# Feeding an encoder layer a second, channel-major copy of its input: no transposes at the start, token sums by matmul, a longer warm-up

## The chip, the cores and the metric

The kernel runs on one core of one Trainium2 chip. The metric is the device time of one execution, in microseconds (us), as the median of several runs. The engines are called TensorE (PE, with its weight loads shown apart as PEld), VectorE (DVE), ScalarE (ACT), GpSimd (POOL) and SyncE (SP), which here issues the DMAs.

## What is computed

One layer of a bidirectional encoder on 256 tokens of 2048 channels. A normalisation, a five-part input projection, a gated recurrence over chunks in both directions, an output projection, and then a gated feed-forward block with a width-3 convolution; each half is added to its input.

```
def reference(x, ...):
    h = rmsnorm(x, norm_pre_mix[i])
    m = hgrn2_mixer(h, hgrn_w_in[j], hgrn_w_out[j], ...)
    x = x + rmsnorm(m, norm_post_mix[i])
    h = rmsnorm(x, norm_pre_ffn[i])
    x = x + rmsnorm(conv_ffn(h, ffn_w_in[i], ffn_w_conv[i], ffn_w_out[i]), norm_post_ffn[i])

def rmsnorm(x, w):
    y = x32 * lax.rsqrt(jnp.mean(x32 * x32, axis=-1, keepdims=True) + EPS)
    return (y * w).astype(x.dtype)
```

All of it is float32. The change concerns the first `rmsnorm` alone: how `x * norm_pre_mix` gets into the layout that the matmuls need, and how the mean square of each token is summed.

## The kernel before, in words

**The work.** The weights, 59 million values, stream from memory once. A product in float32 accuracy is made of fast ones: every weight piece `raw` is split into a rounded part `whi` (a cast on ACT, line 129) and a rest `wlo` (a subtraction on DVE, line 130), every activation likewise into two halves of the tile `xx[:, k, 0/1, :]`. Index `k` counts 16 blocks of 128 channels; the channels of a block lie on the 128 partitions, the 256 tokens along the free side.

**Chunks and steps.** The 2048 by 10240 input weights are taken in chunks of 512 columns. The function `gemm_t` computes a chunk in 8 steps; step `s` uses blocks `k = 2s, 2s+1`. In a step, 8 matmuls multiply `whi` with both halves of `xx` (512 columns, line 206), and 8 multiply `wlo` with the first half (256 columns, line 209). `prep` casts and subtracts the weights some steps ahead: one step in the first chunk, three (`LOOK`) from then on. The chunk's results stand in four PSUM tiles (`pg`) of six that there are, so the second chunk can take two at once, and gets the others when DVE has copied the first chunk's results away (lines 346 and 347).

**The start.** The input `x` arrives with tokens on partitions (`xs`, five DMAs), between the weights of the first chunk, all on SP's queue, in the order `x` 256 columns, weights k 0 and 1, `x` 256, weights k 2 and 3, `x` 512, weights k 4 to 7 (two DMAs), `x` 512, `x` 512, then weights in 1 MB pieces of four blocks. TensorE first does `WARM` = 18 transposes of the identity into a scratch tile. `split_x(k2)` then transposes two blocks of `xs` on TensorE (four 128 by 128 transposes, line 290), multiplies by the norm's weight on ACT (first half, line 294), and takes the rest on DVE (second half, line 298). `split_x(0)` and `split_x(1)` stand ahead of the first chunk; step `s` calls `split_x(s + 2)`.

**The mean square.** ACT squares `xs` and sums along the channels in the same instruction (`square_x`, eight calls, line 309). DVE adds the eight partial sums, GpSimd takes the power -0.5 (`rsqrt_mean`), and `spread` brings the result across the partitions with two matmuls (line 222). The factors `rs1` (per partition) and `r1` (per column) are applied to the results of the projection, not to `xx`. These pieces are put into the list `soon`; each step of a chunk takes one piece from it, so they fall into the second chunk.

**Order.** Each engine runs its instructions in a fixed order. A scheduler makes that order when the program is built, from its own estimate of times; lines marked `keep_in_program_order` keep theirs.

Of the kernel before, what the change touches and what calls it, by code (L numbers as in the profile page):

```python
# [11 lines left out]
F32 = mybir.dt.float32  # L12
F32R = mybir.dt.float32r
U8 = mybir.dt.uint8
AF = mybir.ActivationFunctionType
ALU = mybir.AluOpType
AX = mybir.AxisListType

P = 128
T = 256  # L20
D = 2048
KT = D // P
# [6 lines left out]
EPS = 1e-6  # L29
NLEV = 7  # L30
LOOK = 3
WARM = 18

ORDER = [(s, g) for g in range(NG - 1) for s in "qfbgv"][:-1]
ORDER += [("q", NG - 1), ("f", NG - 1), ("b", NG - 1), ("v", NG - 2), ("g", NG - 1), ("v", NG - 1)]
# [2 lines left out]
C_PRE = 0  # L38
# [8 lines left out]
def encoder_layer(  # L47
    ctx: ExitStack,
    tc: tile.TileContext,
    x: bass.AP,  # L50
    w_in: bass.AP,
    w_o: bass.AP,
    w_up: bass.AP,
# [6 lines left out]
    nc = tc.nc  # L60
    V, S, G = nc.vector, nc.scalar, nc.gpsimd

    def pool(stack, name, bufs=1, **kw):
        return stack.enter_context(tc.tile_pool(name=name, bufs=bufs, **kw))
# [8 lines left out]
    ps_t = pool(ctx, "ps_t", 2, space=bass.MemoryType.PSUM)  # L73

    def stile(n, name):
        return small.tile([P, n], F32, name=name, tag=name)

    prm = const.tile([P, C_END], F32, name="prm")
    ident = const.tile([P, P], F32, name="ident")
    mneg = const.tile([P, 2 * HG], F32, name="mneg")  # L80
    r1 = const.tile([P, T], F32, name="rt", tag="rt")

    x_v = x.rearrange("(m p) d -> p m d", p=P)
    out_v = out.rearrange("(m p) d -> p m d", p=P)


# [15 lines left out]
    def step():  # L102
        if soon or later:
            (soon or later).popleft()()

    def load(pieces=1):
        ci, s = subs[at["load"]]
        wd, c, _ = chunks[ci]
        raw = wraw.tile([P, 4, 512], F32, name="raw", tag="raw")
        src = wd[c, s // 2].rearrange("p (k n) -> p k n", n=512)  # L110
        w = 4 // pieces
        raws[ci, s // 2] = raw
        at["load"] += 2
        for i in range(pieces):
            nc.sync.dma_start(raw[:, w * i : w * i + w], src[:, w * i : w * i + w])
            yield

    def prep(upto):
        while at["prep"] < min(upto, len(subs)):
            i = at["prep"]  # L120
            if at["load"] <= i:
                list(load())
            ci, s = subs[i]
            src = raws[ci, s // 2][:, 2 * (s % 2) : 2 * (s % 2) + 2, :]
            pl, sfx = (extra[0], str(s)) if ci == C_UP - 1 and s >= 2 * chunks[ci][2] - 4 else (wspl, "")
            hi = pl.tile([P, 2, 512], F32R, name="whi", tag="whi" + sfx)
            lo = pl.tile([P, 2, 512], F32R, name="wlo", tag="wlo" + sfx)
            for j in [slice(0, 1), slice(1, 2)] if i == 0 else [slice(0, 2)]:
                S.copy(hi[:, j], src[:, j])  # L129
                V.tensor_tensor(lo[:, j], src[:, j], hi[:, j].bitcast(F32), op=ALU.subtract)  # L130
            parts[ci, s] = (hi, lo)
            at["prep"] += 1
# [3 lines left out]
    def flush():  # L136
        while soon or later:
            step()
# [46 lines left out]
    def gemm_t(xx, need=None, pre=None):  # L185


        ci = at["chunk"]
        at["chunk"] += 1
        nsub = 2 * chunks[ci][2]  # L190
        base = subs.index((ci, 0))
        ps = [ps_g.tile([P, 2, T], F32, name="pg", tag="pg") for _ in range(4)]
        for s in range(nsub):
            if s == need:
                flush()
            if pre:
                pre(s)
            prep(base + s + (LOOK if ci else 1))
            hi, lo = parts[ci, s]


            tiles = [(n, 2 * s + j) for n in range(4) for j in range(2)]
            for run in [tiles] if s < nsub - 1 else [tiles[i : i + 2] for i in range(0, 8, 2)]:
                for n, k in run:
                    w = hi[:, k % 2, n * P : (n + 1) * P]
                    nc.tensor.matmul(ps[n], w, xx[:, k], start=(k == 0), stop=False)  # L206
                for n, k in run:
                    w = lo[:, k % 2, n * P : (n + 1) * P]
                    nc.tensor.matmul(ps[n][:, 0, :], w, xx[:, k, 0, :], start=False, stop=(k == 2 * nsub - 1))  # L209
            step()  # L210
        return ps

    def rsqrt_mean(dst, ss, n):
        V.tensor_scalar(dst, ss, 1.0 / n, EPS, op0=ALU.mult, op1=ALU.add)
        G.tensor_tensor(dst, dst, mneg[:, : dst.shape[1]], op=ALU.pow)

    def spread(rs, name):

        tp = ps_t.tile([P, 2, T], F32, name="tp", tag="tp")
        for m in range(2):  # L220
            a = rs[:, m : m + 1].broadcast_to([P, P])
            nc.tensor.matmul(tp[:, 0, m * P : (m + 1) * P], a, ident, start=True, stop=True)
        S.copy(name, tp[:, 0, :])
# [17 lines left out]
    xx = acts.tile([P, KT, 2, T], F32R, name="xx", tag="xx")  # L241
    hstack = ExitStack()
    sstack = ExitStack()
    spool = pool(sstack, "start", side="right")
    xs = spool.tile([P, 2, D], F32, name="xs")

    def load_x(a, b):
        nc.sync.dma_start(xs[:, :, a:b], x_v[:, :, a:b])

    nc.sync.dma_start(prm[:, :C_CW], par[:, :C_CW])  # L250
    load_x(0, 256)
    first = load(4)
    next(first), next(first)
    load_x(256, 512)
    list(first)
    load_x(512, 1024)
    list(load(2))
    load_x(1024, 1536)
    load_x(1536, 2048)
    make_identity(nc, ident)  # L260
    G.memset(mneg, -0.5)

# [4 lines left out]
    warm = ps_t.tile([P, 2, T], F32, name="tp", tag="tp")  # L267
    for i in range(WARM):
        nc.tensor.transpose(warm[:, 0, :P], ident, ident)
# [13 lines left out]
    V.tensor_scalar(lb1, lb, -1.0, 1.0, op0=ALU.mult, op1=ALU.add)  # L283

    def split_x(k2):
        tp = ps_t.tile([P, 2, T], F32, name="tp", tag="tp")
        for j in range(2):
            k = 2 * k2 + j
            for m in range(2):
                nc.tensor.transpose(tp[:, j, m * P : (m + 1) * P], xs[:, m, k * P : (k + 1) * P], ident)  # L290
        for j in range(2):
            k = 2 * k2 + j
            w1 = prm[:, C_PRE + k : C_PRE + k + 1]
            S.activation(xx[:, k, 0, :], tp[:, j, :], AF.Copy, scale=w1)
        for j in range(2):
            k = 2 * k2 + j
            w1 = prm[:, C_PRE + k : C_PRE + k + 1]
            V.scalar_tensor_tensor(  # L298
                xx[:, k, 1, :], tp[:, j, :], w1, xx[:, k, 0, :].bitcast(F32), op0=ALU.mult, op1=ALU.subtract
            )  # L300

    ss1, rs1 = stile(8, "ss1"), stile(2, "rs1")

    def square_x(q):
        for m in range(2):
            jk = spool.tile([P, 512], F32, name="jk", tag="jk", bufs=2)
            i = 4 * m + q
            c = slice(q * 512, (q + 1) * 512)
            tc.keep_in_program_order(S.activation(jk, xs[:, m, c], AF.Square, accum_out=ss1[:, i : i + 1]))

    def mean_x():
        sx = stile(2, "sx")
        V.tensor_reduce(sx, ss1.rearrange("p (m q) -> p m q", q=4), axis=AX.X, op=ALU.add)
        rsqrt_mean(rs1, sx, D)
        soon.extend([nop, lambda: spread(rs1, r1)])

    split_x(0)
    split_x(1)
    ps0 = gemm_t(xx, pre=lambda s: split_x(s + 2) if 2 * s + 4 < KT else None)
    soon.extend([lambda q=q: square_x(q) for q in range(4)] + [mean_x])  # L320
    ps1 = gemm_t(xx)
    load_rest()
# [209 lines left out]
    ps0 = gemm(oo, need=6)  # L532
# [84 lines left out]
    ps0 = gemm(hh, "head")  # L617
# [58 lines left out]
    ps0 = gemm(gg, need=20)  # L676
# [24 lines left out]
def _lay(inputs):  # L701
    f = lambda n: np.asarray(inputs[n])
    w_in, w_o = f("hgrn_w_in")[0], f("hgrn_w_out")[0]
    w_up, w_dn = f("ffn_w_in")[0], f("ffn_w_out")[0]

    def tiles(w):
        k, n = w.shape
        w = w.reshape(k // 512, 4, P, n // 512, 512).transpose(3, 0, 2, 1, 4)
        return np.ascontiguousarray(w).reshape(n // 512, k // 512, P, 4 * 512)

    cw = f("ffn_w_conv")[0].reshape(3, 2 * FT, P).transpose(2, 1, 0).reshape(P, -1)
    lbd = f("hgrn_lower_bounds")[:, 0].reshape(2, NH, P).transpose(2, 0, 1).reshape(P, -1)
    par = np.concatenate(
        [
            f("norm_pre_mix")[0].reshape(KT, P).T,
            f("norm_pre_ffn")[0].reshape(KT, P).T,
            f("hgrn_gnorm")[0][:, None],
            lbd,
            cw,
        ],  # L720
        axis=1,
    )
    post = np.concatenate([f("norm_post_mix"), f("norm_post_ffn")], axis=0)
    c = np.ascontiguousarray
    return {
        "x": c(f("x")[0]),
        "w_in": tiles(w_in),
        "w_o": tiles(w_o),
        "w_up": tiles(w_up),
        "w_dn": tiles(w_dn),  # L730
        "par": c(par),
        "post": c(post),
        "masks": _masks(),
    }
# [16 lines left out]
```

## Time and profile before

| | us |
|---|---|
| median of 3 runs | 1376.47 (1376.24 to 1377.78) |
| the profiled execution | 1377.04 |
| span of its trace | 1375.3 |
| TensorE busy in it | 1364.0 (99%) |
| VectorE busy | 940.1 (68%) |
| ScalarE busy | 695.0 (51%) |

The span reaches from the first to the last instruction of the core; 1.74 us of the execution's time lie around it. TensorE is busy nearly throughout. "Busy" for its matmuls is a model of pipelined work, so the time between the starts of equal matmuls says more than the duration of one.

### The profile page before, as it was taken

How to read it: one execution, taken by the hardware profiler on the slowest of the kernel's cores; microseconds unless marked ns; L12 is line 12 of the kernel's file. 1: busy time of each engine (PE TensorE's matmuls, PEld its weight loads, DVE VectorE, ACT ScalarE, POOL GpSimd, SP SyncE). 2: the span in 40 equal slices, each digit the busy share in tenths (PEclk: the TensorE clock that was granted, in tenths of full speed). 3: DMA queues.
4: the chain of work that ended last, by engine and by line, in shares of the span. 5: the costliest groups of instructions: out<-in, count | busy, mean ns of one | idle time of the engine just before them, and what ended most of it. 6: DMA issues, size and time to landing. Idle time of an engine off the chain costs nothing.

```text
span 1375.3 us, 18411 instructions
## 1 busy us (share of the span) xinstructions
PE 1364.0 (99%) x7362; PEld 1180.4 (86%) x7362; DVE 940.1 (68%) x1188; ACT 695.0 (51%) x971; POOL 13.5 (1%) x21
## 2 busy tenths in 40 slices
PE   9999999999999999999999999999999999999997
PEld 7888988898898888888888888888888888888886
DVE  5687678866886876567668676877677775444444
ACT  5644454454544444456655555555555554434442
POOL 0000000000000000000000000000000000000000
PEclk9999999999999999999999999999999999999999
DMA  7554355435535444663555555555555555555552
GB/s 282 185 187 150 124 186 181 153 124 186 181 123 184 157 149 153 245 235 109 207 184 183 197 181 203 184 184 185 186 198 183 197 184 214 193 204 183 191 205 94
DMA packets 36998, 248.93 MB, mean 181 GB/s; under 512 B 4144, under 2 KB 4912, under 8 KB 7472
## 3 DMA queue, kind: packets, MB, share of 16 engines
q1 hardware_dynamic: 36912, 247.75, 51.2%
q8 instruction: 58, 0.95, 0.3%
q14 instruction: 28, 0.23, 0.0%
HBM read 245.63 MB, written 2.10 MB: 180 GB/s over the span
## 4 chain that ended last, share of the span: by engine, by line
PE 98%; issue 0%; DMA 0%; DVE 0%; SPq 0%; ACT 0%; DVEq 0%; POOLq 0%; POOL 0%
PE pg L206 36%; PE pg L209 18%; PE pg L178 13%; PE pg L177 13%; PE pg L174 13%; PE sc L435 4%; PE sc L491 1%; PE sc L460 1%; PE sc L492 1%; PE sc L415 1%; DMA xs<-in_x 0%; PE tp L233 0%; PE tp L587 0%; PE tp L290 0%; DVE fw L688 0%
## 5 line engine op out<-in xcount | busy, mean ns | idle before, releaser
L130 DVE TENSOR_TENSOR wlo<-raw,whi 128x1024 fp32r<-128x1024 f32 (+1 forms) x457 | 556.6, 1220 | 364.8 <-ACT whi L129 364.4
L129 ACT CAST whi<-raw 128x1024 fp32r<-128x1024 f32 (+1 forms) x457 | 478.3, 1049 | 508.8 <-PE pg L178 226.1
L206 PE MATMUL pg<-hh,whi 128*128 128x512 f32 x1344 | 355.2, 393 | 0.0
L206 PEld LDWEIGHTS pg<-hh,whi 128*128 128x128 f32 x1344 | 234.1, 189 | 34.7
L209 PEld LDWEIGHTS pg<-hh,wlo 128*128 128x128 f32 x1344 | 197.4, 190 | 22.6
L206 PE MATMUL pg<-xx,whi 128*128 128x512 f32 x768 | 208.6, 399 | 0.1
L209 PE MATMUL pg<-hh,wlo 128*128 128x256 f32 x1344 | 203.3, 281 | 0.0
L206 PEld LDWEIGHTS pg<-xx,whi 128*128 128x128 f32 x768 | 134.6, 190 | 20.2 <-DVE xx L298 0.7
L174 PE MATMUL pg<-whi,gg 128*128 128x512 f32 x352 | 136.9, 389 | 0.0
L177 PE MATMUL pg<-wlo,gg 128*128 128x512 f32 x352 | 136.9, 389 | 0.0
L178 PE MATMUL pg<-whi,gg 128*128 128x512 f32 x352 | 136.9, 389 | 0.0
L209 PEld LDWEIGHTS pg<-xx,wlo 128*128 128x128 f32 x768 | 113.0, 191 | 12.4
L209 PE MATMUL pg<-xx,wlo 128*128 128x256 f32 x768 | 117.4, 283 | 0.0
L177 PE MATMUL pg<-wlo,xx 128*128 128x512 f32 x256 | 101.0, 395 | 0.0
L174 PE MATMUL pg<-whi,xx 128*128 128x512 f32 x256 | 100.2, 391 | 0.0
L178 PE MATMUL pg<-whi,xx 128*128 128x512 f32 x256 | 100.0, 390 | 0.0
L177 PEld LDWEIGHTS pg<-wlo,gg 128*128 128x128 f32 x352 | 66.1, 188 | 13.8
L174 PEld LDWEIGHTS pg<-whi,gg 128*128 128x128 f32 x352 | 66.1, 188 | 13.7
L178 PEld LDWEIGHTS pg<-whi,gg 128*128 128x128 f32 x352 | 66.1, 188 | 13.5
L435 PEld LDWEIGHTS sc<-qs,kc 128*128 128x128 f32 x448 | 57.6, 192 | 1.9
L424 ACT COPY kc<-ks 128x1024 f32<-128x1024 f32 x28 | 32.1, 1147 | 52.4 <-PE sc L435 48.5
L435 PE MATMUL sc<-qs,kc 128*128 128x128 f32 x448 | 58.5, 285 | 0.0
(128 smaller groups left out, 1187.3 us busy)
## 6 DMA issues: line engine op xcount, KB each, us to landing
raw<-in_w_up SPq DMA_DIRECT2D x88, 1024.0 KB, 4.9
raw<-in_w_in SPq DMA_DIRECT2D x78, 1024.0 KB, 4.9
raw<-in_w_dn SPq DMA_DIRECT2D x44, 1024.0 KB, 4.9
raw<-in_w_o SPq DMA_DIRECT2D x16, 1024.0 KB, 4.9
x<-in_x SPq DMA_DIRECT2D x1, 2048.0 KB, 7.9
wp<-in_post SPq DMA_DIRECT2D x2, 1024.0 KB, 5.7
out<-fw SPq DMA_DIRECT2D x8, 256.0 KB, 2.6
xs<-in_x SPq DMA_DIRECT2D x3, 512.0 KB, 9.9
```

The source lines that it names most:

```text
L129: S.copy(hi[:, j], src[:, j])
L130: V.tensor_tensor(lo[:, j], src[:, j], hi[:, j].bitcast(F32), op=ALU.subtract)
L174: mm = nc.tensor.matmul(ps[m], a, hi[:, j, :], start=(k == 0), stop=False)
L177: nc.tensor.matmul(ps[m], a, lo[:, j, :], start=False, stop=False)
L178: nc.tensor.matmul(ps[m], b, hi[:, j, :], start=False, stop=(k == 2 * nsub - 1))
L206: nc.tensor.matmul(ps[n], w, xx[:, k], start=(k == 0), stop=False)
L209: nc.tensor.matmul(ps[n][:, 0, :], w, xx[:, k, 0, :], start=False, stop=(k == 2 * nsub - 1))
L415: nc.tensor.matmul(sc[:, j, :], kc[0][:, h, sl], q[:, h, sl], start=True, stop=True)
L424: S.copy(kc[0].rearrange("p h (n two m) -> p (h n) two m", two=2, m=m), halves(ks, m))
L435: nc.tensor.matmul(sc[:, j, :], kc[0][:, h, sl], r, start=True, stop=True)
L460: nc.tensor.matmul(sc[:, h, :], ks[:, d, h, s0 : s0 + P], qs[:, 1 - d, h, t0 : t0 + P], start=True, stop=True)
L491: nc.tensor.matmul(o[:, h, :], Sd[:, 2 * h + b, :], v[:, b, cs], start=True, stop=False)
```

## The change

A second input `xt` holds `x` by channels: partition `p` has, for each block `k`, the 256 tokens of channel `128 k + p`. `xs` is loaded from it in the same five places of SP's queue, with as many bytes. `split_x` becomes a multiplication on ACT and one on DVE, straight from `xs`, with no transposes. It is called for step `s + 1` in step `s`. The squares are made in place, four blocks at a time; DVE sums them over `k` in five reductions that read `xs` with a stride of 256 elements; and two matmuls with a column of ones (`one`) sum over the partitions. In the first step of the first chunk the matmuls are sorted by `k`. `WARM` is 24.

```
-WARM = 18
+WARM = 24
...
             tiles = [(n, 2 * s + j) for n in range(4) for j in range(2)]
+            if ci == s == 0:
+                tiles.sort(key=lambda nk: nk[1])
...
-    xs = spool.tile([P, 2, D], F32, name="xs")
+    xs = spool.tile([P, KT, T], F32, name="xs")
     def load_x(a, b):
-        nc.sync.dma_start(xs[:, :, a:b], x_v[:, :, a:b])
+        nc.sync.dma_start(xs[:, a:b], xt_v[:, a:b])
...
     def split_x(k2):
+        for k in (2 * k2, 2 * k2 + 1):
+            S.activation(xx[:, k, 0, :], xs[:, k, :], AF.Copy, scale=prm[:, C_PRE + k : C_PRE + k + 1])
+        for k in (2 * k2, 2 * k2 + 1):
+            w1, hi = prm[:, C_PRE + k : C_PRE + k + 1], xx[:, k, 0, :].bitcast(F32)
+            V.scalar_tensor_tensor(xx[:, k, 1, :], xs[:, k, :], w1, hi, op0=ALU.mult, op1=ALU.subtract)
+
+    ss1, rs1 = spool.tile([P, 5, T], F32, name="ss1"), stile(2, "rs1")
+    one = stile(1, "one")
+    G.memset(one, 1.0)
+
+    def square_x(q):
+        k = slice(4 * q, 4 * q + 4)
+        tc.keep_in_program_order(S.activation(xs[:, k], xs[:, k], AF.Square))
+        V.tensor_reduce(ss1[:, q, :], xs[:, k].rearrange("p k t -> p t k"), axis=AX.X, op=ALU.add)
+
+    def mean_x():
+        V.tensor_reduce(ss1[:, 4, :], ss1[:, :4].rearrange("p q t -> p t q"), axis=AX.X, op=ALU.add)
         tp = ps_t.tile([P, 2, T], F32, name="tp", tag="tp")
...
         for m in range(2):
+            nc.tensor.matmul(tp[:, 0, m : m + 1], ss1[:, 4, m * P : (m + 1) * P], one, start=True, stop=True)
+        rsqrt_mean(rs1, tp[:, 0, :2], D)
         soon.extend([nop, lambda: spread(rs1, r1)])
     split_x(0)
-    split_x(1)
-    ps0 = gemm_t(xx, pre=lambda s: split_x(s + 2) if 2 * s + 4 < KT else None)
+    ps0 = gemm_t(xx, pre=lambda s: split_x(s + 1) if 2 * s + 2 < KT else None)
```

**Where instructions moved.** First TensorE, from its first instruction on, before the change: L269 is the warm-up, L290 the transposes of `x`, L206 and L209 the `whi` and `wlo` matmuls of steps 0 to 3.

```order
L269 MATMUL tp<-ident 128x128 x18
L290 MATMUL tp<-ident,xs 128x128 x8
L206 MATMUL pg<-xx,whi 128x512 x8
L209 MATMUL pg<-xx,wlo 128x256 x8
L206 MATMUL pg<-xx,whi 128x512 x8
L290 MATMUL tp<-ident,xs 128x128 x8
L209 MATMUL pg<-xx,wlo 128x256 x8
L206 MATMUL pg<-xx,whi 128x512 x4
L290 MATMUL tp<-ident,xs 128x128 x4
L206 MATMUL pg<-xx,whi 128x512 x4
L209 MATMUL pg<-xx,wlo 128x256 x8
```

The same place with the change, where lines 210 and 213 are what 206 and 209 were:

```order
L273 MATMUL tp<-ident 128x128 x24
L210 MATMUL pg<-xx,whi 128x512 x8
L213 MATMUL pg<-xx,wlo 128x256 x8
L210 MATMUL pg<-xx,whi 128x512 x8
L213 MATMUL pg<-xx,wlo 128x256 x8
L210 MATMUL pg<-xx,whi 128x512 x8
L213 MATMUL pg<-xx,wlo 128x256 x8
```

The first eight transposes of `x` stood ahead of every real matmul, the next ones between the matmuls; now only the warm-up does.

Second, ACT from its start, before: L129 casts weights (two halves, then whole steps 1 to 3), L294 makes the first half of `xx`.

```order
L278 ACT_TABLE_LOAD
L278 ACTIVATE lex<-lex 128x32
L129 CAST whi<-raw 128x512 x2
L294 ACTIVATE xx<-tp,prm 128x256 x4
L129 CAST whi<-raw 128x1024 x3
L294 ACTIVATE xx<-tp,prm 128x256 x6
L129 CAST whi<-raw 128x1024 x2
```

And with the change (L131 is the cast, L291 the first half of `xx`):

```order
L282 ACT_TABLE_LOAD
L282 ACTIVATE lex<-lex 128x32
L291 ACTIVATE xx<-xs,prm 128x256 x2
L131 CAST whi<-raw 128x512 x2
L291 ACTIVATE xx<-xs,prm 128x256 x2
L131 CAST whi<-raw 128x1024
L291 ACTIVATE xx<-xs,prm 128x256 x4
L131 CAST whi<-raw 128x1024 x2
L291 ACTIVATE xx<-xs,prm 128x256 x8
L131 CAST whi<-raw 128x1024 x7
```

The first two blocks of `xx` moved ahead of the first casts; blocks 4 to 7 now stand ahead of the casts of steps 2 and 3, and blocks 8 to 15 ahead of that of step 4.

Third, DVE where the second chunk begins, before: L347 copies the first chunk's results away, L130 subtracts weights, L313 and L214 belong to the mean square.

```order
L130 TENSOR_TENSOR wlo<-raw,whi 128x1024 x2
L347 TENSOR_TENSOR qT<-pg,qT 128x256 x3
L130 TENSOR_TENSOR wlo<-raw,whi 128x1024
L347 TENSOR_TENSOR qT<-pg,qT 128x256
L130 TENSOR_TENSOR wlo<-raw,whi 128x1024 x2
L313 TENSOR_REDUCE sx<-ss_136 128x2
L214 TENSOR_SCALAR rs_137<-sx 128x2
```

And with the change (L132 is the subtraction, L342 the copying away, L303 and L306 the reductions, L218 what L214 was):

```order
L303 TENSOR_REDUCE ss_142<-xs 128x256
L342 TENSOR_TENSOR qT<-pg,qT 128x256 x3
L132 TENSOR_TENSOR wlo<-raw,whi 128x1024
L303 TENSOR_REDUCE ss_142<-xs 128x256
L342 TENSOR_TENSOR qT<-pg,qT 128x256
L132 TENSOR_TENSOR wlo<-raw,whi 128x1024
L303 TENSOR_REDUCE ss_142<-xs 128x256
L132 TENSOR_TENSOR wlo<-raw,whi 128x1024
L306 TENSOR_REDUCE ss_142<-ss_142 128x256
L132 TENSOR_TENSOR wlo<-raw,whi 128x1024 x3
L218 TENSOR_SCALAR rs_143<-tp 128x2
```

The first reduction stands ahead of the copying away, the next ones between the weights' subtractions (a further L303 and L132 stand between the seventh row and the eighth's like, and are not repeated).

## Rows read from the trace of the kernel before

**Rows 1.** The page's first lines, and the table of stretches (columns: length, busy time and count of PE, PEld, DVE, ACT, POOL, granted TensorE clock, DMA share, GB/s).

```profile
span 1375.3 us, 18411 instructions
PE 1364.0 (99%) x7362; PEld 1180.4 (86%) x7362; DVE 940.1 (68%) x1188; ACT 695.0 (51%) x971; POOL 13.5 (1%) x21
0.00:100.00 100.00, 96.92 (x525) 84.24 (x526) 67.81 (x95) 56.06 (x86) 1.46 (x8) 1.00 0.61 220
100.00:200.00 100.00, 100.00 (x595) 88.76 (x594) 72.65 (x86) 50.40 (x74) 2.02 (x2) 1.00 0.43 152
...
1200.00:1300.00 100.00, 100.00 (x443) 82.84 (x442) 46.22 (x39) 40.08 (x41) 0.00 (x0) 1.00 0.55 190
```

**Rows 2.** The timeline of PE over the first 31 us (columns: start, us, engine, line, operation, tiles, shapes, count, and in brackets the idle time before it with what ended it).

```profile
1.36 4.10 PE L269 MATMUL tp<-ident 128*128 128x128 f32 x18 [1.36 <-POOL ident masks.py:199]
5.25 1.06 PE L290 MATMUL tp<-ident,xs 128*128 128x128 f32 x4
7.95 1.09 PE L290 MATMUL tp<-ident,xs 128*128 128x128 f32 x4 [1.63 <-DMA xs<-in_x]
9.06 3.78 PE L206 MATMUL pg<-xx,whi 128*128 128x512 f32 x8
12.64 1.80 PE L209 MATMUL pg<-xx,wlo 128*128 128x256 f32 x8
14.27 2.01 PE L206 MATMUL pg<-xx,whi 128*128 128x512 f32 x8
16.12 1.03 PE L290 MATMUL tp<-ident,xs 128*128 128x128 f32 x8
16.91 1.20 PE L209 MATMUL pg<-xx,wlo 128*128 128x256 f32 x8
18.17 1.19 PE L206 MATMUL pg<-xx,whi 128*128 128x512 f32 x4
...
25.11 2.09 PE L206 MATMUL pg<-xx,whi 128*128 128x512 f32 x8
...
31.22 2.68 PE L206 MATMUL pg<-xx,whi 128*128 128x512 f32 x11
```

**Rows 3.** The timeline of PE in the second chunk, in a plain step and around the two matmuls of `spread` (L222).

```profile
45.20 2.00 PE L206 MATMUL pg<-xx,whi 128*128 128x512 f32 x8
47.04 1.12 PE L209 MATMUL pg<-xx,wlo 128*128 128x256 f32 x8
47.99 2.00 PE L206 MATMUL pg<-xx,whi 128*128 128x512 f32 x8
...
55.42 1.11 PE L209 MATMUL pg<-xx,wlo 128*128 128x256 f32 x8
56.37 0.60 PE L222 MATMUL tp<-ident,rs 128*128 128x128 f32 x4
56.73 0.70 PE L206 MATMUL pg<-xx,whi 128*128 128x512 f32 x2
```

**Rows 4.** The timeline of ACT: casts of weights for steps 0 (first half), 2, 3, and 4 with 5.

```profile
5.20 0.62 ACT L129 CAST whi<-raw 128x512 fp32r<-128x512 f32 x1 [1.96 <-DMA raw<-in_w_in]
13.09 1.04 ACT L129 CAST whi<-raw 128x1024 fp32r<-128x1024 f32 x1 [2.25 <-DMA raw<-in_w_in]
14.38 1.06 ACT L129 CAST whi<-raw 128x1024 fp32r<-128x1024 f32 x1 [0.24 <-DMA raw<-in_w_in]
20.56 2.00 ACT L129 CAST whi<-raw 128x1024 fp32r<-128x1024 f32 x2
```

**Rows 5.** DMA issues of `x` and of weights, each with the time from issue to landing on the line below it: `x` pieces 1, 3 and 5 (the last), then the weights of steps 4 and 5 (their count, median duration of the issue in ns, and start in us).

```profile
L248 SPq DMA_DIRECT2D xs<-in_x x1: 423/423/423, 1.2 to 1.2; - x1
DMA to landing us min/median/max: 2.6/2.6/2.6
L248 SPq DMA_DIRECT2D xs<-in_x x1: 434/434/434, 4.1 to 4.1; - x1
DMA to landing us min/median/max: 7.7/7.7/7.7
L248 SPq DMA_DIRECT2D xs<-in_x x1: 379/379/379, 7.1 to 7.1; - x1
DMA to landing us min/median/max: 9.9/9.9/9.9
L115 SPq DMA_DIRECT2D raw<-in_w_in x1: 340/340/340, 7.8 to 7.8; - x1
DMA to landing us min/median/max: 11.7/11.7/11.7
```

**Rows 6.** The table of stretches again, in pieces of 2 us (columns as in rows 1).

```profile
4.00:6.00 2.00, 2.00 (x11) 1.91 (x9) 0.60 (x4) 0.62 (x1) 0.00 (x0) 1.00 0.63 178
10.00:12.00 2.00, 2.00 (x6) 1.53 (x5) 1.94 (x3) 0.84 (x1) 0.00 (x0) 1.00 0.99 393
18.00:20.00 2.00, 1.94 (x11) 1.57 (x11) 1.29 (x4) 0.49 (x2) 0.00 (x0) 1.00 1.02 423
```

**Rows 7.** Groups of instructions by form (columns: line, engine, operation, tiles, shapes, count | busy us, mean ns of one | idle before), the first two of the first 35 us, the others of the second chunk.

```profile
L298 DVE SCALAR_TENSOR_TENSOR xx<-tp,prm,xx 128x256 fp32r<-128x256 f32 x16 | 6.9, 478 | 3.8 <-ACT xx L294 3.8
L294 ACT ACTIVATE xx<-tp,prm 128x256 fp32r<-128x256 f32 x16 | 6.6, 472 | 5.2 <-PE tp L290 5.2
L130 DVE TENSOR_TENSOR wlo<-raw,whi 128x1024 fp32r<-128x1024 f32 x11 | 13.5, 1224 | 11.5 <-ACT whi L129 11.5
L347 DVE TENSOR_TENSOR qT<-pg,qT 128x256 f32<-128x256 f32 x4 | 1.6, 421 | 0.7 <-ACT qT L346 0.5
L379 DVE TENSOR_SCALAR ks<-f 128x1024 f32<-128x1024 f32 x1 | 0.7, 686 | 0.0
```

More of the change, by code (lines that the diff above doesn't have):

```diff
@@ L50, in encoder_layer @@
     x: bass.AP,
+    xt: bass.AP,
     w_in: bass.AP,
@@ L83, in encoder_layer @@
     x_v = x.rearrange("(m p) d -> p m d", p=P)
+    xt_v = xt.rearrange("p (k t) -> p k t", t=T)
     out_v = out.rearrange("(m p) d -> p m d", p=P)
@@ L244, in encoder_layer @@
     spool = pool(sstack, "start", side="right")
-    xs = spool.tile([P, 2, D], F32, name="xs")
+    xs = spool.tile([P, KT, T], F32, name="xs")
     def load_x(a, b):
-        nc.sync.dma_start(xs[:, :, a:b], x_v[:, :, a:b])
+        nc.sync.dma_start(xs[:, a:b], xt_v[:, a:b])
     nc.sync.dma_start(prm[:, :C_CW], par[:, :C_CW])
-    load_x(0, 256)
+    load_x(0, 2)
     first = load(4)
     next(first), next(first)
-    load_x(256, 512)
+    load_x(2, 4)
     list(first)
-    load_x(512, 1024)
+    load_x(4, 8)
     list(load(2))
-    load_x(1024, 1536)
-    load_x(1536, 2048)
+    load_x(8, 12)
+    load_x(12, 16)
     make_identity(nc, ident)
@@ L285, in split_x @@
     def split_x(k2):
-        tp = ps_t.tile([P, 2, T], F32, name="tp", tag="tp")
[L287 to L300, printed above, removed]
@@ L302, in encoder_layer @@
-    ss1, rs1 = stile(8, "ss1"), stile(2, "rs1")
-    def square_x(q):
-        for m in range(2):
[L306 to L314, printed above, removed]
+        for k in (2 * k2, 2 * k2 + 1):
+            S.activation(xx[:, k, 0, :], xs[:, k, :], AF.Copy, scale=prm[:, C_PRE + k : C_PRE + k + 1])
@@ L726, in _lay @@
         "x": c(f("x")[0]),
+        "xt": c(f("x")[0].reshape(T, KT, P).transpose(2, 1, 0)).reshape(P, -1),
         "w_in": tiles(w_in),
```

## The prediction

> **What bounds the kernel now.** I read the page first, then stretches of 100 us. TensorE is busy for 1364.0 of 1375.3 us, and in the stretches from 100 us to 1300 us for all of it; only the first stretch has idle time, 3.1 us [rows 1]. So a microsecond of TensorE's time saved at the start is saved at the end, as long as nothing later makes TensorE wait. The other engines matter only where TensorE waits for them.
>
> Then the timeline of TensorE at the start [rows 2]. The warm-up starts at 1.36 and the first transposes of `x` at 5.25, so 18 warm-up transposes take 3.89 us, 0.216 each. A second group of transposes waits until 7.95 for `x`, and the first real matmul starts at 9.06. Step 0 lasts from 9.06 to 14.27 (5.21 us). A plain step lasts 47.99 - 45.20 = 2.79 us [rows 3]. The same eight `whi` matmuls are 3.58 us apart from their successors at 9.06 and 1.85 at 14.27, almost twice: until about 14 us TensorE runs at the lower of its two clocks, 1.2 GHz, and then at 2.4, after 5.2 us of real matmuls and about five of transposes with a gap of 1.63 us between. The column of the granted clock reads 1.00 even there [rows 6], so here I trust the paces.
>
> From there, steps 2 to 5 run from 18.17 to 31.22, 13.05 us where four plain steps are 11.16; the 1.89 between them are 16 transposes of `x`, at some 0.11 each. Eight such transposes at 16.12 took 0.79 us, 0.10 each.
>
> Last the other side, the supply. From 8 to 22 us the DMA engines are full, near 400 GB/s [rows 6]. Weights of step 2 land at 13.09 and of step 3 at 14.38, when ACT, which waited for them, casts them [rows 4]; those of steps 4 and 5 land at 7.8 + 11.7 = 19.5 [rows 5]. TensorE comes to step 4 only at 25.11 [rows 2]. So before the change TensorE lags its weights by more than 4 us there: that is what can be won, and the landing times cap it.
>
> **The change, part by part, in the order of time.**
>
> *First matmul.* Nothing of `x` on TensorE stands ahead of it; the warm-up does. It now ends at 1.36 + 24 x 0.216 = 6.55. The other inputs are earlier: the first half cast ends at 5.20 + 0.62 = 5.82 [rows 4], `x` piece 1 lands at 1.2 + 2.6 = 3.8 [rows 5], and one block of `xx` takes ACT 6.6/16 = 0.41 and DVE 6.9/16 = 0.43 [rows 7], so it is there by 4.7. These rows are for sources in PSUM; from SBUF I take the same, since the cast of 512 elements from SBUF takes 0.62. First matmul at 6.6, not 9.06.
>
> *Steps 0 and 1.* If the clock rises as it did, 5.2 us after the first matmul, step 0 ends at 6.6 + 5.2 = 11.8 and step 1 at 14.6. The page "TensorE: Matmul & The Clock Gate" of the Trainium skill (Part 4, PE-mode transpose) says that the full clock does not engage for transposes; this speaks against a longer warm-up. The trace of before neither confirms nor contradicts it, since its transposes are broken by the gap. By it, the six added transposes cost 1.3 us at the first matmul and give nothing back.
>
> If on the contrary the unbroken warm-up raises the clock, step 0 lasts 2.8 us and TensorE is through step 1 by about 13. It changes little, because step 2 has another condition: ACT first makes blocks 4 to 7 of `xx`, whose `x` lands at 4.1 + 7.7 = 11.8, so until 11.8 + 4 x 0.41 = 13.4, then casts the weights that landed at 13.09, until about 14.5. **Step 2 starts at 14.6 either way**, not at 18.17.
>
> *Steps 2 to 5.* Two plain steps end at 14.6 + 5.58 = 20.2. ACT has cast step 3 by 15.6, then makes eight blocks of `xx` (3.3 us, and the last `x` is there at 7.1 + 9.9 = 17.0), done by 18.9. The weights of step 4 land at 19.5; their cast takes 1.05 (two in 2.00 at 20.56). **Step 4 starts at 20.6**, a wait of 0.4 us that takes the place of part of the gain, and steps 4 and 5 end at 26.2. Before, that point was 31.22. Gain 5.0 us.
>
> *The sums over tokens.* In place of nothing, TensorE gets two matmuls with one column. Nearest row: the two of `spread` move the next matmul from 0.95 us after the `wlo` group's start (47.04 to 47.99) to 1.31 (55.42 to 56.73), so 0.18 each [rows 3]; a load of 128 weights is in both. Bounds: 0.10 each (a transpose above) and 0.36 (twice the row). I take 0.36 for both, ends 0.2 and 0.7.
>
> *The reductions on DVE.* Five, each reading 1024 elements at a stride. Bounds: 0.69 us, the one-source operation of that size (L379), and twice the two-source one, 2.45; I take 1.22 (L130) [rows 7]. With ACT's squares gone from eight calls to four, only DVE is loaded more. It must, between the subtraction for step 2 of the second chunk (its cast starts when step 7 frees a tile, at 26.2 + 2.79 = 29.0, and takes 1.05, so about 30.1) and the sum over tokens in its step 6 (26.2 + 2 x 2.79 + 6 x 2.79 + 1.2 = 49.7), do five subtractions (6.1), four copyings (1.7) and five reductions: 19.6 us of room, 13.9 of work at 1.22. Hidden. What waits behind the first reduction is the copying away, for which the second chunk's last two PSUM tiles wait; a cast and a square on ACT end at 31.1, DVE reduces until about 32.6 and copies three times until 33.9. TensorE starts the second chunk at 31.8 and does three and a half half-steps of 1.4 first, until 36.7. Hidden too. The cover is gone at 2.4 us for a reduction.
>
> *The loads.* SP issues them in the same places with the same bytes, in pieces of twice the length. From 4 to 6 us, mostly the short pieces of `x`, the queues moved 178 GB/s at a share of 0.63, later 423 at 1.02 [rows 6]: 283 against 415 GB/s for a full share. So nothing is lost; at best the first 5 MB come 1 us earlier. I count 0 and keep 1 for the range.
>
> **Sum.** -5.0 + 0.36 = -4.65 us, against the profiled execution's 1377.04 (span 1375.3 and 1.74 around it): 1372.4. That execution lay 0.57 above the median; part of this may be chance at the start, part chance everywhere. I take the middle between 1372.4 and 1371.8: 1372.1.
>
> **The rivals.**
>
> *Supply comes earlier.* Longer pieces let step 4's weights land up to 1 us before 19.5, and then a clock raised in the warm-up counts as well. Gain up to 6.0 - 0.36: 1370.8. For it: the low GB/s at 4 to 6 us. Against: from 12 us the queues moved nearly 400 with the old pieces.
>
> *Part of the gain goes.* The clock rises later than 5.2 us after the first matmul, each further step at 1.2 GHz costing 5.2 - 2.8 = 2.4 us, or reductions near 2.4 to 3 us make TensorE wait for the sums. 1373.4 to 1375.
>
> *No change.* If TensorE waited for weights anyway, the removed transposes would only lengthen that wait. That needs landings at TensorE's own pace; at step 4 it lags them by 25.11 - 20.6 = 4.5 us, so this speaks against it. 1376.5.
>
> *Slower: the strided reductions.* They stand ahead of subtractions whose weights TensorE needs. The room of 19.6 us is used up at 2.36 us each; every microsecond above costs five, and the gain of 4.65 is gone at 2.36 + 0.93 = 3.3 us. At 4 us each: 5 x 4 + 7.8 - 19.6 = 8.2 of waiting, 1380.6. For it: no row shows a long or a strided reduction. Against: all two-source rows of this size are at 1.22.
>
> **How the numbers follow.** Likeliest case 0.60, its own range 1371.2 to 1373.2 (bounds of the matmuls, a landing 0.4 us either way, the median's offset). Earlier supply 0.14. Part of the gain goes 0.16. No change 0.05, slower 0.05. A measurement of this kernel can tell about 0.2%, 2.75 us, from no change. Faster takes the first two and most of the third, 0.86; same takes a fourth of the third and the fourth, 0.09; slower 0.05. The range 1370.5 to 1374.0 leaves out about 2 in 10.
>
> **What would show it.** In the trace of after: first real matmul near 6.6, step 2 near 14.6, step 4 near 20.6 with ACT waiting for DMA just before its cast, step 6 near 26.2; then TensorE without a gap, the two one-column matmuls adding 0.36, and reductions of about 1.2 us. The `whi` pace in steps 0 and 1 shows whether the longer warm-up raised the clock. The prediction is wrong if the reductions take above 2.4 us, if TensorE idles in the second chunk, or if the weights of step 4 land elsewhere than near 19.5.

## The result, and the profile after

The changed kernel takes 1380.33 us (median of 12 runs, 1379.58 to 1381.59), the kernel before 1376.88 beside it (12 runs, 1376.12 to 1377.86): 1.0026 times as long, interval 1.0019 to 1.0034. It is slower by 3.5 us, where 4.4 less were forecast. The profiled execution of after took 1380.53 us.

The start went as forecast. The timeline of TensorE in after (start in us, duration of the group, tiles, and in brackets what ended the idle time), to be held against [rows 2]:

```profile
1.39 4.21 PE L273 MATMUL tp<-ident 128*128 128x128 f32 x24 [1.39 <-POOL ident masks.py:199]
6.27 1.20 PE L210 MATMUL pg<-xx,whi 128*128 128x512 f32 x4 [0.67 <-ACT whi L131]
14.59 2.13 PE L210 MATMUL pg<-xx,whi 128*128 128x512 f32 x8 [0.75 <-ACT whi L131]
...
20.76 2.13 PE L210 MATMUL pg<-xx,whi 128*128 128x512 f32 x8 [0.30 <-ACT whi L131]
...
26.46 2.03 PE L210 MATMUL pg<-xx,whi 128*128 128x512 f32 x8
```

Step 6 begins at 26.46 and not at 31.22: 4.8 us have been won. The cast for step 4 waits for its weights, as forecast (timeline of ACT):

```profile
19.66 2.00 ACT L131 CAST whi<-raw 128x1024 fp32r<-128x1024 f32 x2 [0.55 <-DMA raw<-in_w_in]
```

The token sums, in the second chunk (timelines of DVE and TensorE), cost TensorE only the time of their own loads and columns (each of the two matmuls stands as two records in the trace):

```profile
30.75 2.01 DVE L303 TENSOR_REDUCE ss<-xs 128x256 f32<-128x1024 f32 x1
48.87 1.33 PE L210 MATMUL pg<-xx,whi 128*128 128x512 f32 x5
50.04 0.50 PE L309 MATMUL tp<-one,ss 128*128 128x1 f32 x4
50.40 0.94 PE L210 MATMUL pg<-xx,whi 128*128 128x512 f32 x3
```

So at 60 us the kernel is still more than 4 us ahead. It is behind at the end, and nothing waits in between. The page and the stretches of 100 us (busy time of PE, PEld, DVE, ACT, POOL with the count of instructions, granted clock, DMA share, GB/s), as in [rows 1]:

```profile
span 1378.8 us, 18356 instructions
PE 1366.3 (99%) x7340; PEld 1171.0 (85%) x7340; DVE 948.5 (69%) x1192; ACT 694.3 (50%) x959; POOL 12.4 (1%) x22
...
0.00:100.00 100.00, 95.66 (x519) 81.78 (x520) 79.07 (x102) 57.50 (x76) 1.49 (x9) 1.00 0.64 229
100.00:200.00 100.00, 100.00 (x592) 87.95 (x592) 72.12 (x86) 49.38 (x74) 2.02 (x2) 1.00 0.43 146
200.00:300.00 100.00, 100.00 (x568) 86.83 (x567) 73.13 (x86) 48.09 (x70) 1.56 (x2) 1.00 0.44 155
```

TensorE is busy for 100 us in every 100, at a granted clock of 1.00. What differs is the count. The third stretch of before holds eight matmuls more:

```profile
200.00:300.00 100.00, 100.00 (x576) 88.12 (x575) 74.37 (x84) 47.64 (x69) 1.01 (x1) 1.00 0.46 158
```

Each matmul takes longer, then, and only some do. One view of single tiles shows which (duration min/median/max in ns, start of the first and of the last in us). The tile named last is the stationary operand, the other one streams. The rows of line 174 (176 in after) are those of the function `gemm`, which the change does not touch: `whi` or `wlo` streams in 512 columns, against `xx` in a part of the input projection, `oo` in the output projection and `gg` in the feed-forward block's last product. The `hh` row is the block's first product, by `gemm_t`, where the weights are stationary. Before:

```profile
L174 PE MATMUL pg<-whi,xx x256: 389/389/492, 82.0 to 535.1; 128*128 128x512 f32 x128
L174 PE MATMUL pg<-whi,oo x128: 387/389/478, 535.8 to 631.3; 128*128 128x512 f32 x128
L206 PE MATMUL pg<-hh,whi x1344: 387/395/478, 656.6 to 1127.1; 128*128 128x512 f32 x192
L174 PE MATMUL pg<-whi,gg x352: 389/389/396, 1127.6 to 1366.3; 128*128 128x512 f32 x176
```

And after:

```profile
L176 PE MATMUL pg<-whi,xx x256: 389/396/488, 71.4 to 536.1; 128*128 128x512 f32 x128
L176 PE MATMUL pg<-whi,oo x128: 389/395/480, 536.8 to 634.3; 128*128 128x512 f32 x128
L210 PE MATMUL pg<-hh,whi x1344: 389/394/482, 660.0 to 1130.6; 128*128 128x512 f32 x192
L176 PE MATMUL pg<-whi,gg x352: 389/389/398, 1131.0 to 1369.8; 128*128 128x512 f32 x176
```

(The first `xx` matmul of `gemm` has an earlier place in after's order.) The last one is 1.0 us later than before, the last `oo` 3.0, the first `hh` of the large stage 3.4, and from there to the end the lag stays at 3.4 to 3.5. The median of the `xx` and `oo` matmuls is 6 to 7 ns longer; that of `gg` is the same. The duration of an overlapped matmul is a model, so the starts decide. `gemm` issues three matmuls per weight block, and nine of them lie between these pairs, before and then after (timeline of single instructions):

```profile
82.43 0.39 PE L178 MATMUL pg<-whi,xx 128*128 128x512 f32 x1
84.48 0.39 PE L178 MATMUL pg<-whi,xx 128*128 128x512 f32 x1
```

```profile
81.70 0.40 PE L179 MATMUL pg<-wlo,xx 128*128 128x512 f32 x1
83.80 0.40 PE L179 MATMUL pg<-wlo,xx 128*128 128x512 f32 x1
```

2.05 against 2.10 us. Over the whole stages, the mean from a matmul's start to the next one's (the "pace" below; the few intervals above 300 ns are left out) is 227.1 ns before and 233.2 after for `xx` (768 matmuls, +4.7 us), 227.1 and 232.6 for `oo` (384, +2.1 us), 226.7 in both for `gg`. Another 96 in `gemm` with `hh` as the stationary tile add 0.4: 7.2 us in sum.

### The profile page after: what moved, and what is told of

Its sections match the earlier page's. It is cut to its first block, busy times and chain, and to the rows that moved or that the text cites. A ratio compares the mean times of both kernels' runs of the same rounds, so it can differ in the third digit from the quotient of the medians.

```text
span 1378.8 us, 18356 instructions
## 1 busy us (share of the span) xinstructions
PE 1366.3 (99%) x7340; PEld 1171.0 (85%) x7340; DVE 948.5 (69%) x1192; ACT 694.3 (50%) x959; POOL 12.4 (1%) x22
## 4 chain that ended last, share of the span: by engine, by line
PE 98%; DMA 1%; issue 0%; DVE 0%; ACT 0%; SPq 0%; DVEq 0%; POOLq 0%; POOL 0%; ACTq 0%
PE pg L210 35%; PE pg L213 18%; PE pg L176 13%; PE pg L179 13%; PE pg L180 13%; PE sc L430 4%; DMA raw<-in_w_in 1%; PE sc L487 1%; PE sc L486 1%; PE sc L455 1%; PE sc L410 1%; DMA xs<-in_xt 0%; PE tp L237 0%; PE tp L582 0%; DVE fw L683 0%
## 5 line engine op out<-in xcount | busy, mean ns | idle before, releaser
L132 DVE TENSOR_TENSOR wlo<-raw,whi 128x1024 fp32r<-128x1024 f32 (+1 forms) x457 | 556.5, 1221 | 361.1 <-ACT whi L131 357.9
L131 ACT CAST whi<-raw 128x1024 fp32r<-128x1024 f32 (+1 forms) x457 | 477.6, 1048 | 513.6 <-PE pg L180 223.0
L210 PEld LDWEIGHTS pg<-hh,whi 128*128 128x128 f32 x1344 | 233.1, 188 | 36.1
```

## The experiments

**Theory.** The matmul is the same instruction with the same shapes; only addresses differ. The change drops the tiles `ss1` (32 bytes a partition) and `sx` from the pool `small` and adds `one`; each takes 32 bytes there in the built program. So `raw`, `whi`, `wlo` and the other tiles above it lie 32 bytes lower (`whi` at 44736 and not 44768), while `xx`, `hh` (196576) and `oo` (163040), allocated from the other end, stay. `gg` lies above `whi` and moves with it. Let D be how far `whi` has moved towards higher addresses relative to `xx`, in bytes: 0 before, -32 after. (Before, the addresses of `whi` and `xx` differ by a multiple of 256.) The theory: D sets the pace, and the change itself is worth about what was forecast. The rival: something in the change itself, such as the new layout of `x`, the reductions or the order of instructions, slows the later stages.

The median times of all runs are in one table at the end of this section; paces are worked out from the starts in each trace. The kernel before was measured again beside each group of runs; its medians there lie between 1376.47 and 1376.88.

**Put the 32 bytes back.** In the pool `small` of the changed kernel, ahead of `prm`, a tile that nothing uses:

```
+    stile(8, "gap")
```

> The changed kernel with one unused tile of 32 bytes in the pool `small`, so that the weight tiles whi and wlo stand again at the addresses that they have in the kernel before (whi 44768 instead of 44736). No instruction differs. Theory A (address: the matmuls of the function gemm, with xx or oo as weights and whi or wlo streaming, run slower because the change moved whi by 32 bytes against xx): their start-to-start time returns from 232 to 235 ns to 227 ns, 6.8 us come back over 70 to 670 us, and the kernel takes 1373.5 us, 3.4 us faster than before. Theory B (the changed order on DVE and TensorE after the start costs the time): 1380.3, as the changed kernel.

1372.59 us, 0.9971 of before (0.9959 to 0.9983): 7.74 us less than after, by an unused tile. The tile view:

```profile
L177 PE MATMUL pg<-whi,xx x256: 388/389/492, 70.9 to 530.6; 128*128 128x512 f32 x128
L177 PE MATMUL pg<-whi,oo x128: 387/389/479, 531.3 to 626.8; 128*128 128x512 f32 x128
```

The medians are 389 again, and the lead of 4.5 us is kept (the last `xx` matmul is at 530.6 where before has 535.1). Two starts nine matmuls apart are 2.04 us apart:

```profile
82.03 0.39 PE L181 MATMUL pg<-whi,xx 128*128 128x512 f32 x1
84.07 0.39 PE L181 MATMUL pg<-whi,xx 128*128 128x512 f32 x1
```

In both programs TensorE's instructions have the same order, so the two traces can be laid side by side: after is 0.5 us behind at its first `gemm` matmul (that much was lost by 26 us, while weights were still awaited), 7.5 us at the last `oo` matmul, and 7.9 to 8.0 from the large `hh` stage to the end. The loss thus arises almost wholly in `gemm`.

The trace of after holds a comparison of its own. The last 48 matmuls of the output projection, from 623.17 us on, take `whi` and `wlo` from another pool (line 127, `extra`), at addresses that the change leaves as they were, so that D is 0 for them. The pace goes at that place from 233.4 ns (the 336 matmuls ahead) to 226.8 (the 32 until other work comes between); in before it is 227.1 and 226.7. Two pairs nine matmuls apart, 2.10 and 2.04 us:

```profile
620.14 0.40 PE L180 MATMUL pg<-whi,oo 128*128 128x512 f32 x1
622.24 0.40 PE L180 MATMUL pg<-whi,oo 128*128 128x512 f32 x1
623.63 0.39 PE L180 MATMUL pg<-whi,oo 128*128 128x512 f32 x1
625.67 0.39 PE L180 MATMUL pg<-whi,oo 128*128 128x512 f32 x1
```

**The same in the kernel before**, one line, D = +32:

```
+    stile(8, "gap")
```

> The kernel before with the same unused 32 bytes, which move whi the other way, to 44800. Theory A, if only the address modulo 64 bytes counts: the gemm matmuls go from 227 to about 233 ns and the kernel takes 6.8 us more, 1383.7. Theory A, if the sign of the shift matters: anything between. Theory B: 1376.9, unchanged.

1388.43 us, 1.0084 of before (1.0067 to 1.0101). An unused tile of 32 bytes makes the old kernel 12.0 us slower (1376.48 beside it); its pace with `xx` is 233.4 ns, with `oo` 232.7. The rival falls: the slow pace needs nothing of the change. The paces account for most of the time: 768 x 6.3 + 384 x 5.6 ns in `gemm` are 7.0 us, and in `gemm_t` (2112 pairs, at the paces of the `hh` stage) the `whi` matmuls are 2.3 ns slower and the `wlo` ones 0.3 faster, 4.2 us; together 11.2 of the 12.0.

**96 bytes**, D = +64:

```
+    stile(24, "gap")
```

> The changed kernel with 96 unused bytes: whi at 44832, 64 bytes above where the kernel before has it. Theory A with a period of 64 bytes: as with 32 bytes, 1373.5 us and 227 ns. Theory A with a period of 128 bytes or more: near 1380 us and 232 to 235 ns. Theory B: 1380.3.

1369.86 us, 0.995 of before. `gemm` is not at its best here (229.2 ns), but the feed-forward block's first product, where `hh` streams and the weights are stationary, is faster than at 0, -32 or +32:

```profile
706.40 1.07 PE L214 MATMUL pg<-hh,wlo 128*128 128x256 f32 x8
```

Its `wlo` matmuls come every 114.3 ns (118.5 before), and the stage from the first to the last `hh` matmul of line 211 takes 466.8 us where before took 470.5.

**Distance or address?** Here `whi` stays at 44736 as in after, and a tile of 32 bytes behind `xx` moves `xx`, `hh` and `oo` down by as much: D = 0.

```
+    acts.tile([P, 8], F32, name="gap", tag="gap")
```

> The changed kernel with 32 unused bytes at the other end of the memory: xx, hh and oo move down by 32 bytes, whi stays at 44736, so the distance between whi and xx is that of the kernel before while whi's own address is the changed one. Theory A, distance counts: 1373.5 us and 227 ns. Theory A', whi's own address counts (a start that is no odd multiple of 32 bytes is slow): 1380 us and 232 to 235 ns. Theory B: 1380.3.

1372.49 us, with all paces as with the 32 bytes put back. So it is the distance between the two tiles, not where `whi` lies.

**Other distances.** Four sizes of the same unused tile in the changed kernel: `stile(40, "gap")` (D = +128), `stile(32, "gap")` (+96), `stile(72, "gap")` (+256), `stile(56, "gap")` (+192).

> The changed kernel with 160 unused bytes, so that whi stands 128 bytes above its place in the kernel before. If the distance between whi and xx counts modulo 128 bytes, this is the run with 32 bytes again: 227 ns for the gemm matmuls, 118.6 ns for the wlo matmuls of gemm_t, 1372.6 us. If it counts modulo 64 bytes, the same (but the run with 96 bytes speaks against 64 already). If it counts modulo 256 or more: other paces, between 1368 and 1381 us.

> The changed kernel with 128 unused bytes: whi 96 bytes above its place in the kernel before. Modulo 128 this is the changed kernel's own distance (32 below): 1380.3 us, 232 to 235 ns in gemm. Modulo 64 it is the distance of the kernel before with 32 bytes: near 1384 us or more. With a longer period neither is expected.

> The changed kernel with 288 unused bytes: whi 256 bytes above its place in the kernel before. If the distance counts modulo 256 bytes, this is the run with 32 bytes again: 227 ns for the gemm matmuls, 1372.6 us. If the period is longer: 229 to 234 ns, 1370 to 1384 us.

> The changed kernel with 224 unused bytes: whi 192 bytes above its place in the kernel before, which modulo 256 is 64 below. If only the size of the distance counts, the paces are those of 64 above: 229 ns in gemm, 114.3 ns for wlo in gemm_t, 1369.9 us. If its sign counts: others, 1370 to 1384 us.

At +128 the kernel takes 1382.15 us, at +96 1384.72: +128 is not 0 again and +96 is not -32, so the paces do not repeat after 128 bytes. At +256 everything is as at 0 (1372.67 us, pace 227.1). At +192 the size of the distance is 64 again, modulo 256, but with the other sign; I expected the time of +64 if only the size counts, and got 1372.97 and a pace of 233.3. The sign counts. With +192 the slow `gemm` is made up for by `gemm_t`: its `whi` matmuls come every 229.4 ns and its `wlo` ones every 116.6, 231.0 and 118.5 before.

**Is the gain of the change the same at another distance?** The kernel before with `stile(16, "gap")`, D = +64.

> The kernel before with 64 unused bytes, at the distance between whi and xx of the changed kernel with 96 bytes (1369.9 us). If address and change are independent, the gain of the change is the same at this distance as at the other (1376.5 to 1372.6, 3.9 us): 1369.9 + 3.9 = 1373.8 us. If the change itself slows the later matmuls in some way beside the address: something else.

1373.68 us. At D = +64 the change is worth 1373.68 - 1369.86 = 3.8 us, at D = 0 it is 1376.48 - 1372.59 = 3.9. The two effects add.

**The warm-up.** The changed kernel at D = 0 with the old warm-up:

```
+    stile(8, "gap")
...
-WARM = 24
+WARM = 18
```

> The changed kernel at the addresses of before (32 unused bytes) with 18 warm-up transposes instead of 24: the worth of the longer warm-up. If the start is bound by the landings, as the prediction has it: first matmul near 5.9 us, step 4 still near 20.6, and 1372.6 us, within 0.5 us of the run with 24. If the longer warm-up is what raises the clock early: the lower clock in steps 0 and 1, step 2 later than 14.6, and up to 2 us more.

1372.45 us, no different from 1372.59. The timelines of TensorE, with 24 transposes and then with 18:

```profile
6.88 2.11 PE L211 MATMUL pg<-xx,whi 128*128 128x512 f32 x8 [1.10 <-ACT whi L132]
...
20.27 2.11 PE L211 MATMUL pg<-xx,whi 128*128 128x512 f32 x8 [0.27 <-ACT whi L132]
```

```profile
6.43 3.78 PE L211 MATMUL pg<-xx,whi 128*128 128x512 f32 x8 [0.94 <-ACT whi L132]
14.46 2.11 PE L211 MATMUL pg<-xx,whi 128*128 128x512 f32 x8 [0.18 <-ACT whi L132]
20.56 2.11 PE L211 MATMUL pg<-xx,whi 128*128 128x512 f32 x8 [0.24 <-ACT whi L132]
```

The first eight real matmuls take 3.78 us and not 2.11, at the lower clock, and step 4 still starts at 20.56 against 20.27, since it waits for its weights in both. The longer warm-up buys nothing here.

**Two attempts at the best of both.** First, at D = 0, another distance for `wlo` alone: 64 bytes between `whi` and `wlo`, and 192 more ahead of `gg`, so that `gg` keeps its distance to `whi` modulo 256.

```
+    stile(8, "gap")
...
+            if i == 0:
+                wspl.tile([P, 16], F32, name="gap2", tag="gap2", bufs=1)
...
+    gpool.tile([P, 48], F32, name="gap3")
```

> The changed kernel with three unused tiles: 32 bytes in `small`, 64 bytes between whi and wlo, and bytes ahead of gg. whi stands then as in the kernel before (231.0 ns for its 512-column matmuls in gemm_t, 227.1 in gemm), wlo 64 bytes above (114.3 ns for its 256-column ones, 229.2 in gemm). If each weight tile's own distance sets the pace of its own matmuls: a step of gemm_t is 8 x (231.0 + 114.3) = 2762 ns instead of 2796, 264 steps, so 9.0 us less than the run with 32 bytes, and a third of 1504 gemm matmuls 2.1 ns slower, 1.6 us with gg: 1365.2 us. If the distance of the next load to the matmul that runs counts instead, the paces are others, and the time lies between 1366 and 1373 us.

It failed: 1381.29 us, 1.0034 of before.

```profile
L179 PE MATMUL pg<-whi,gg x352: 387/395/398, 1126.3 to 1370.6; 128*128 128x512 f32 x176
```

All three paces of `gemm` rose (`xx` 231.9, `oo` 231.5, `gg` 232.0), those of the `whi` matmuls too, whose own distance had not changed; over 768, 384 and 1056 matmuls that is 11.0 us, and `gemm_t` gave back 2.3 (both paces fell, by 0.3 and 0.8 ns), which makes up the 8.7 us against 1372.59. So a matmul's pace does not depend on its own two operands alone; in `gemm`, `whi` and `wlo` matmuls alternate.

Second, D = +64 with `oo` alone brought back to 0 (modulo 256):

```
+    stile(24, "gap")
...
+    opool.tile([P, 48], F32, name="gap2")
```

> The run with 96 bytes (1369.9 us), with unused bytes that bring oo back to its distance of before from whi, modulo 256 bytes. If the distance counts modulo 256 and for each pair of tiles by itself: the matmuls with oo go from 229.0 to 227.1 ns, 384 of them, 0.7 us less, 1369.1 us, and no other pace changes. With a longer period: 229 to 233 ns with oo, up to 1.5 us more.

1368.89 us (1368.80 to 1368.96), 0.9946 of before (0.9931 to 0.996). The output projection with +64 and then with 0:

```profile
L177 PE MATMUL pg<-whi,oo x128: 387/394/481, 531.7 to 627.9; 128*128 128x512 f32 x128
```

```profile
L177 PE MATMUL pg<-whi,oo x128: 387/389/487, 531.2 to 626.7; 128*128 128x512 f32 x128
```

96.2 and 95.5 us from first to last, 0.7 less, and the pace of `oo` is 227.2 ns; the rest is as it was. The median is 1.0 us lower. This is the fastest version run.

All together, sorted by D (median us; paces in ns: `gemm` with `xx`, with `oo`; `gemm_t` in the `hh` stage, `whi` and `wlo`). `gg` is at 226.7 in all but the split one.

| D | kernel | us | `xx` | `oo` | `whi` | `wlo` |
|---|---|---|---|---|---|---|
| -32 | after | 1380.33 | 233.2 | 232.6 | 232.5 | 116.9 |
| 0 | before | 1376.88 | 227.1 | 227.1 | 231.0 | 118.5 |
| 0 | after + 32 bytes | 1372.59 | 227.1 | 227.1 | 231.0 | 118.4 |
| 0 | after, `xx` side moved | 1372.49 | 227.1 | 227.1 | 231.0 | 118.4 |
| 0 | after + 32 bytes, warm-up 18 | 1372.45 | 227.1 | 227.1 | 231.0 | 118.5 |
| +32 | before + 32 bytes | 1388.43 | 233.4 | 232.7 | 233.3 | 118.2 |
| +64 | before + 64 bytes | 1373.68 | 229.2 | 229.0 | 232.3 | 114.3 |
| +64 | after + 96 bytes | 1369.86 | 229.2 | 229.0 | 232.4 | 114.3 |
| +64, `oo` 0 | after + 96 bytes, `oo` moved | 1368.89 | 229.2 | 227.2 | 232.4 | 114.3 |
| +96 | after + 128 bytes | 1384.72 | 233.4 | 232.8 | 233.7 | 117.9 |
| +128 | after + 160 bytes | 1382.15 | 232.4 | 231.9 | 233.0 | 118.4 |
| +192 | after + 224 bytes | 1372.97 | 233.3 | 232.7 | 229.4 | 116.6 |
| +256 | after + 288 bytes | 1372.67 | 227.1 | 227.1 | 231.0 | 118.5 |
| 0, `wlo` +64 | split | 1381.29 | 231.9 | 231.5 | 230.7 | 117.6 |

## Why the prediction was wrong

**The step that failed** is the one in the first paragraph: that a microsecond of TensorE's time saved at the start is saved at the end, as long as nothing later makes TensorE wait. Nothing later made it wait, and of the 4.8 us ahead at step 6 none was left at the end: TensorE's own matmuls became slower, in stages that the change does not touch, since tiles there had moved by 32 bytes. "Busy 100%" was read as a fixed amount of work. In the forecast's sum the term that is missing is +7.74 us, what the 32 bytes cost (1380.33 - 1372.59).

**The working of the change itself held.** With distances as before, it is worth 3.9 us by the medians and 4.5 between the two traces; 4.65 were forecast, and the time of 1372.59 lies 0.5 from the 1372.1 forecast.

- First matmul: 6.27 in after (6.6 forecast). Step 2: 14.59 (14.6). Step 4: 20.76 (20.6), after a wait of ACT for the weights. Step 6: 26.46 (26.2).
- The two one-column matmuls: the eight matmuls of line 210 around them start 50.40 - 48.87 = 1.53 us apart for five, which at 0.231 each take 1.16: 0.37 (0.36 forecast).
- The reductions were mis-sized: 2.0 us each and not 1.22. The forecast had put the loss of cover at 2.36, so it stayed hidden, with less to spare than was said.
- The warm-up: the forecast left open whether it raises the clock and gave it no value, since the landings cap step 2. Both sides of that are seen: in after the clock rose in the warm-up, and with 18 transposes the total is the same.

**The slower rival** had the sign and nearly the time (1380.6), by a mechanism that did not occur: TensorE never waited for a reduction. That is luck and no confirmation.

**Of the rule weighed there**, from "TensorE: Matmul & The Clock Gate" of the Trainium skill (Part 4, PE-mode transpose), that the full clock does not engage for transposes, the traces say the opposite for these. In after, the 24 take 4.21 us where 24 x 0.216 would be 5.18: about the first half start 0.21 apart, the others 0.11, with nothing but transposes before. TensorE went from 1.2 to 2.4 GHz during the warm-up.

What stays open: which accesses collide. The runs show that the distance decides; that it repeats after 256 bytes is shown at 0 and +256, and for `oo` alone, but at no other pair. The split run shows that a matmul's own operands are not the whole of it. The load of the next weights, which overlaps the streaming (PEld is busy 85% of the span), is one candidate, and the work of ACT and DVE in SBUF is another (no `xx` matmul of `gemm` in these traces is without some within 0.25 us); no run here takes them apart. Transfers are not the cause: the `xx` matmuls of `gemm` with no DMA packet in flight within 0.25 us of them come every 233.1 ns in after (196 of them) and every 226.9 before (187).

## What to carry to other kernels

Where one engine is busy all the time, compare the starts of equal instructions in stages that the change does not touch: a change that adds or drops a small tile moves every tile above it, and here 32 bytes cost twice what the change gained. Before an edit of less than 1% is judged, list the addresses of the large tiles with and without it and restore their distances with an unused tile, which here was enough modulo 256 bytes. Then try a few distances on purpose, stage by stage: they gave 3.7 us beyond the change itself (1372.59 to 1368.89).

## What the hardware showed that was not expected

The pace of the 512-column matmuls of `gemm`, at the full clock and with nothing waiting, ranged from 227.1 to 233.4 ns with the distance between the tiles in SBUF, that of the 256-column ones of `gemm_t` from 114.3 to 118.5. Of the distances tried, `gemm` was fastest where both `whi` and `wlo` differ from `xx` by a multiple of 256 bytes, `gemm_t` at +64 or +192.

TensorE's clock, once risen in a warm-up, could fall again. In the kernel before with 32 bytes more, the transposes' spacing halves at 5.8 us; then TensorE idles for 2.36 us, waiting for `x`, and its first eight real matmuls are 12.68 - 9.16 = 3.52 us long, 0.44 each, the lower clock (timeline of TensorE; then stretches of 2 us, where the granted clock is the third value from the end):

```profile
8.48 0.63 PE L291 MATMUL tp<-ident,xs 128*128 128x128 f32 x4 [2.36 <-DMA xs<-in_x]
9.16 3.69 PE L207 MATMUL pg<-xx,whi 128*128 128x512 f32 x8
12.68 1.11 PE L210 MATMUL pg<-xx,wlo 128*128 128x256 f32 x8
```

```profile
8.00:10.00 2.00, 1.47 (x6) 1.16 (x7) 1.45 (x3) 1.45 (x5) 0.00 (x0) 0.80 1.02 343
10.00:12.00 2.00, 2.00 (x6) 1.52 (x6) 1.93 (x3) 0.91 (x1) 0.00 (x0) 0.50 1.04 382
12.00:14.00 2.00, 2.00 (x13) 1.80 (x12) 0.17 (x1) 0.00 (x0) 0.00 (x0) 0.85 1.02 394
```

After's warm-up leads into the matmuls with a gap of 0.67 us, and the clock stays up. When it rises differs between executions: in the kernel before, with the same warm-up of 18, the real matmuls come at the slow pace from 9.06 us to about 14 [rows 2]; what decides is not shown.
